# Encoder kernel on one core: the loading and splitting of x in another order, two blocks to a PSUM bank, two load queues

## The chip, the cores and the metric

The kernel runs on one core of a Trainium2 chip. The metric is the device time of one execution in microseconds; the time before is the median of three runs. The engines go by the names of the profile: PE is TensorE (PEld its weight loads), ACT is ScalarE, DVE is VectorE, POOL is GpSimd, SP is SyncE, which here issues most DMA transfers.

## The reference, cut to what matters

A two-layer encoder on 256 tokens of 1024 features, all in float32. Each layer is a half-step SwiGLU, a mixer (windowed attention beside a convolution module), a second half-step SwiGLU, and a gated embedding. The change touches only the very start of layer 0: x comes in, is scaled by the gain of the first norm and goes into the first SwiGLU product.

```python
def rms_norm(x, g, eps=1e-6):
    y = x * lax.rsqrt(jnp.mean(x * x, axis=-1, keepdims=True) + eps)
    return y * g

def swiglu(x, w_in, w_out):
    gate, up = jnp.split(x @ w_in, 2, axis=-1)
    return (jax.nn.silu(gate) * up) @ w_out

for i in range(DEPTH):
    h = x + 0.5 * swiglu(rms_norm(x, norm_ffn1[i]), w_ffn1_in[i], w_ffn1_out[i])
    ...
```

## The kernel before

**Layout.** Activations are kept transposed, features on the 128 partitions and the 256 tokens along the row. The 1024 features of x make eight blocks of 128 (`KD` = 8), counted 0 to 7. `x32` keeps x in float32 for the residual sum.

**Products.** Each matrix product is made of three: an operand is split into a high part and a low part, both in the float32r form of TensorE, and `mm3` (lines 311 to 313) adds high x high, low x high and high x low for every block. So x becomes `x0h` (ACT: x times the gain, rounded) and `x0l` (DVE: x times the gain minus `x0h`). A weight tile of 128 x 1024 goes through the same: it lands as `raw`, ACT casts it to `w_hi` (line 100), DVE subtracts to make `w_lo` (line 101). The factor 1/rms is applied after the product, so the products don't wait for it.

**Weights.** `Weights` loads units of 0.5 or 1 MB on SP's queue (line 76) into four `raw` buffers, and prepares tiles ahead of their use into seven `w_hi`/`w_lo` pairs. The incoming x (`x_ld`) takes one of the four `raw` buffers until its last block has been transposed. The first four units are 0.5 MB, one tile each; the units after them are 1 MB, two tiles each.

**The start.** x comes as four quarters of 256 columns (two blocks each) on SP's queue (line 166); the gains `rows_first` come on ACT's queue (line 180). TensorE transposes the gains into `ps_par`, and ACT copies them to `par`. Then, for each block: two transposes into PSUM (`ps_xt`, line 461), `x0h` on ACT (line 464), `x0l` on DVE (line 465); and two blocks later `keep_x` copies the block from PSUM to `x32` (line 456, ACT and DVE in turn). Each block has a PSUM tile of its own. The squares of x are summed on ACT and POOL (lines 396 to 400, `sq_acc`) and one matmul adds them over the partitions (`ps_stat`, line 409), after which 1/rms is made and the finished products may leave PSUM.

**What sets the order.** A scheduler orders each engine's instructions by priority and its own estimate of time, except where the code forbids it: in the block of line 450 ACT and DVE keep the order in which the code is written (`manual_schedule`). TensorE's order there is the scheduler's. Within one PSUM tile the framework makes an engine that writes wait for the engines that read, whichever part of the tile they use.

**The first product group.** It is "fresh": `pair` runs blocks 0 to 6 with the first tile (21 matmuls), blocks 0 to 6 with the second, and then block 7 with both (6 matmuls). PSUM has two pools: `mm_tile`, four tiles of one bank, and `at_tile`, two tiles of two banks.

Of the kernel before, what the change touches and what calls it, by code (L numbers as in the profile page):

```python
# [9 lines left out]
F32 = mybir.dt.float32  # L10
F32R = mybir.dt.float32r
AF = mybir.ActivationFunctionType
ALU = mybir.AluOpType
AX = mybir.AxisListType

P = 128
T = 256
D = 1024
KD = D // P
# [119 lines left out]
def encoder_kernel(ctx: ExitStack, tc: tile.TileContext, a: dict, out: bass.AP):  # L139
    nc = tc.nc  # L140
# [11 lines left out]
    def mm_tile(name):  # L152
        return mmp.tile([P, 512], F32, name=name, tag="mm")
# [5 lines left out]
    ident = const.tile([P, P], F32, name="ident")  # L159
    make_identity(nc, ident)  # L160

    x_ld = raw_pool.tile([P, 2, D], F32, name="x_ld", tag="raw")
    xv = a["x"][0].rearrange("(t p) d -> p t d", p=P)
    for i in range(4):
        s = slice(i * 256, (i + 1) * 256)
        nc.sync.dma_start(x_ld[:, :, s], xv[:, :, s])

    col = {}
    par = const.tile([P, 96], F32, name="par")
# [13 lines left out]
    def place_params(tile_, rows, c0):  # L183
        r0 = 0
        for name in rows:
            n = 1 if name in ("q_norm", "k_norm") else a[name].shape[1] // P
            col[name] = (c0 + r0, n)
            r0 += L * n
        ps = at_tile("ps_par")
        nc.tensor.transpose(ps[:, :r0], tile_[:r0, :], ident[:r0, :r0])  # L190
        nc.scalar.copy(out=par[:, c0 : c0 + r0], in_=ps[:, :r0])
        return c0 + r0
# [5 lines left out]
    ws = Weights(tc, raw_pool, w_pool)  # L198
# [101 lines left out]
    def pcol(name, l, k):  # L300
        c0, n = col[name]
        return par[:, c0 + l * n + k : c0 + l * n + k + 1]
# [32 lines left out]
    x32 = xp.tile([P, KD, T], F32, name="x32", tag="x32")  # L335
# [114 lines left out]
    with tc.manual_schedule(engines={mybir.EngineType.Activation, mybir.EngineType.DVE}):  # L450
        n_par = place_params(rows_first, ("norm_ffn1",), 0)
        xT = {}

        def keep_x(k):
            copy = nc.scalar.copy if k % 2 else nc.vector.tensor_copy
            copy(out=x32[:, k, :], in_=xT[k])  # L456

        for k in range(KD):
            xT[k] = (mm_tile if 2 <= k < 6 else at_tile)("ps_xt")[:, :T]
            for t in range(2):  # L460
                nc.tensor.transpose(xT[k][:, t * P : (t + 1) * P], x_ld[:, t, k * P : (k + 1) * P], ident)
            gain = pcol("norm_ffn1", 0, k)
            xh, xl = (x[:, k, :] for x in x_cur)
            nc.scalar.activation(out=xh, in_=xT[k], func=AF.Copy, scale=gain)
            nc.vector.scalar_tensor_tensor(
                out=xl, in0=xT[k], scalar=gain, in1=xh.bitcast(F32), op0=ALU.mult, op1=ALU.subtract
            )
            if k >= 2:
                keep_x(k - 2)
        ws.prep_upto(0)  # L470
        keep_x(KD - 2)
        keep_x(KD - 1)
        ws.prep_upto(1)
        for k in range(KD):
            stat.add(x32[:, k, :])
    r_cur = stat.finish(5)
# [599 lines left out]
```

## Time and profile before

| | us |
|---|---|
| median of three runs (1176.48 to 1177.78) | 1177.25 |
| the profiled execution | 1176.52 |
| its span, first to last instruction | 1174.7 |
| PE busy | 1156.8 (98%) |
| DVE busy | 813.6 (69%) |
| ACT busy | 614.2 (52%) |
| POOL busy | 88.5 (8%) |
| first product group starts | 10.76 |

Times in the trace count from the span's start. In the list of waits a row reads: who waited, for whom, us in total, how often, the longest. In the chain a row reads: start, length, what. In the timeline: start, length, engine, line, operation, output<-inputs, size, how many were merged, and in brackets how long the engine was idle before it and what ended that. Matmuls overlap, so their spacing is the difference of two starts, and not the length of one. The granted clock reads 1.00 throughout.

### The profile page before, as it was taken

What the parts mean: (1) busy time and instruction counts of PE and PEld (TensorE: products, weight loads), DVE (VectorE), ACT (ScalarE), POOL (GpSimd) and SP (SyncE); (2) the same over time, 40 slices, a digit from 0 to 9 for tenths busy, and PEclk for the clock granted to TensorE, in tenths of its full rate; (3) what the DMA queues carried; (4) which work ended last, traced back from release to release, by engine and by line L of the source; (5) the groups of instructions that cost most, each with busy time, mean ns of one, the idle gap of its engine ahead of it and who ended that gap; (6) DMA issues with size and microseconds to landing.
All of it is one profiled execution on the core that took longest, in us unless ns stands there. A gap on an engine that the chain in (4) does not pass through costs nothing.

```text
span 1174.7 us, 21809 instructions
## 1 busy us (share of the span) xinstructions
PE 1156.8 (98%) x9082; PEld 1121.5 (95%) x9082; DVE 813.6 (69%) x1214; ACT 614.2 (52%) x1033; POOL 88.5 (8%) x119
## 2 busy tenths in 40 slices
PE   7999999999999999999999999999999999999997
PEld 7999999998889999999999999999987999999997
DVE  5866656798667766656876666569976786666564
ACT  6644444676356544444664444457753564444443
POOL 3000001211002000001110000113000010000110
PEclk9999999999999999999999999999999999999999
DMA  8866556545074565556556464566522664654541
GB/s 252 265 229 209 167 178 200 179 147 141 2 249 161 189 200 175 171 165 214 188 166 204 156 205 152 170 213 193 145 72 68 219 224 159 201 168 144 192 144 37
DMA packets 195694, 202.99 MB, mean 173 GB/s; under 512 B 3731, under 2 KB 188899, under 8 KB 195596
## 3 DMA queue, kind: packets, MB, share of 16 engines
q1 hardware_dynamic: 195564, 201.60, 53.6%
q8 instruction: 71, 1.16, 0.4%
q14 instruction: 27, 0.22, 0.1%
q10 hardware_dynamic: 32, 0.01, 0.0%
HBM read 200.53 MB, written 1.06 MB: 172 GB/s over the span
## 4 chain that ended last, share of the span: by engine, by line
PE 96%; DVE 2%; DMA 1%; ACT 1%; issue 0%; SPq 0%; ACTq 0%
PE ps_gu L313 14%; PE ps_gu L311 14%; PE ps_gu L312 14%; PE ps_fo L313 7%; PE ps_fo L312 7%; PE ps_fo L311 7%; PE ps_g L311 3%; PE ps_g L313 3%; PE ps_g L312 3%; PE ps_co L847 2%; PE ps_s L755 1%; PE ps_c L311 1%; PE ps_pe L313 1%; PE ps_pe L312 1%; PE ps_pe L311 1%; PE ps_c L313 1%
## 5 line engine op out<-in xcount | busy, mean ns | idle before, releaser
L101 DVE TENSOR_TENSOR w_lo<-raw,w_hi 128x1024 fp32r<-128x1024 f32 (+1 forms) x368 | 440.9, 1202 | 241.5 <-ACT w_hi L100 237.4
L100 ACT CAST w_hi<-raw 128x1024 fp32r<-128x1024 f32 (+1 forms) x368 | 377.2, 1030 | 427.0 <-PE ps_gu L312 215.3
L313 PE MATMUL ps_fo<-h_hi,w_lo 128*128 128x256 f32 x704 | 198.6, 283 | 0.0
L312 PE MATMUL ps_fo<-h_lo,w_hi 128*128 128x256 f32 x704 | 198.6, 283 | 0.0
L311 PE MATMUL ps_fo<-h_hi,w_hi 128*128 128x256 f32 x704 | 198.6, 283 | 0.0
L313 PEld LDWEIGHTS ps_fo<-h_hi,w_lo 128*128 128x128 f32 x704 | 134.9, 192 | 0.0
L311 PEld LDWEIGHTS ps_fo<-h_hi,w_hi 128*128 128x128 f32 x704 | 134.9, 192 | 0.0
L312 PEld LDWEIGHTS ps_fo<-h_lo,w_hi 128*128 128x128 f32 x704 | 134.9, 192 | 0.0
L400 POOL TENSOR_TENSOR sq_acc<-sq_acc,sq 128x256 f32<-128x256 f32 x56 | 56.5, 1010 | 903.4 <-ACT sq L399 902.9
L311 PE MATMUL ps_gu<-x0h,w_hi 128*128 128x256 f32 x352 | 100.8, 286 | 2.1 <-ACT x L456 2.1
L607 DVE SCALAR_TENSOR_TENSOR y<-cpad,cw,y 128x256 f32<-128x256 f32 x240 | 101.1, 477 | 0.1
L313 PE MATMUL ps_gu<-x0h,w_lo 128*128 128x256 f32 x352 | 100.4, 285 | 0.2 <-DVE w_lo L101 0.2
L312 PE MATMUL ps_gu<-x0l,w_hi 128*128 128x256 f32 x352 | 100.2, 285 | 0.0
L311 PE MATMUL ps_gu<-xn0h,w_hi 128*128 128x256 f32 x352 | 99.8, 284 | 0.0
L312 PE MATMUL ps_gu<-xf0l,w_hi 128*128 128x256 f32 x352 | 99.8, 284 | 0.0
L312 PE MATMUL ps_gu<-xf1l,w_hi 128*128 128x256 f32 x352 | 99.8, 284 | 0.0
L311 PE MATMUL ps_gu<-xf0h,w_hi 128*128 128x256 f32 x352 | 99.7, 283 | 0.0
L311 PE MATMUL ps_gu<-xf1h,w_hi 128*128 128x256 f32 x352 | 99.7, 283 | 0.0
L313 PE MATMUL ps_gu<-xf0h,w_lo 128*128 128x256 f32 x352 | 99.6, 283 | 0.0
L313 PE MATMUL ps_gu<-xn0h,w_lo 128*128 128x256 f32 x352 | 99.6, 283 | 0.0
L312 PE MATMUL ps_gu<-xn0l,w_hi 128*128 128x256 f32 x352 | 99.6, 283 | 0.0
L313 PE MATMUL ps_gu<-xf1h,w_lo 128*128 128x256 f32 x352 | 99.6, 283 | 0.0
(222 smaller groups left out, 2718.6 us busy)
## 6 DMA issues: line engine op xcount, KB each, us to landing
raw<-in_w_ffn_in_dram SPq DMA_DIRECT2D x86, 1024.0 KB
raw<-in_w_in_dram SPq DMA_DIRECT2D x30, 1024.0 KB
raw<-in_w_ffn_out_dram SPq DMA_DIRECT2D x32, 896.0 KB
raw<-in_w_ffn_out_dram SPq DMA_DIRECT2D x16, 1024.0 KB
raw<-in_w_o_dram SPq DMA_DIRECT2D x8, 1024.0 KB
raw<-in_w_pe_gate_dram SPq DMA_DIRECT2D x8, 1024.0 KB
raw<-in_w_attn_out_dram SPq DMA_DIRECT2D x8, 512.0 KB
raw<-in_w_conv_out_dram SPq DMA_DIRECT2D x4, 1024.0 KB
```

What stands on the lines that cost most here:

```text
L100: nc.scalar.copy(out=hv[:, :, d0 : d0 + w], in_=src),
L101: nc.vector.tensor_tensor(out=lv[:, :, d0 : d0 + w], in0=src, in1=hv[:, :, d0 : d0 + w].bitcast(F32), op=ALU.subtract,),
L311: nc.tensor.matmul(ps, wh[:, k0 + k, cols], xh[:, kx, :], start=f, stop=False)
L312: nc.tensor.matmul(ps, wh[:, k0 + k, cols], xl[:, kx, :], start=False, stop=False)
L313: nc.tensor.matmul(ps, wl[:, k0 + k, cols], xh[:, kx, :], start=False, stop=e)
L400: nc.gpsimd.tensor_tensor(out=self.acc, in0=self.acc, in1=sq, op=ALU.add)
L607: nc.vector.scalar_tensor_tensor(out=y[:, i, :], in0=src, scalar=w, in1=y[:, i, :], op0=ALU.mult, op1=ALU.add)
L755: nc.tensor.matmul(ps[:, c, :], qT[v * HD : (v + 1) * HD, c, qb * P : (qb + 1) * P], kT[v * HD : (v + 1) * HD, :], start=True, stop=True,)
L847: nc.tensor.matmul(ps[:, c * T : (c + 1) * T], w[:, k, c * P : (c + 1) * P], x[:, k, :], start=k == 0, stop=k == KC - 1,)
```

## The change

Three edits, all ahead of the first product. (1) Quarters 0 and 2 of x are loaded on SP's queue, quarters 1 and 3 on ACT's, where `rows_first` now stands behind them. (2) Two blocks share a one-bank PSUM tile: blocks 0 and 1, 2 and 3, 4 and 5, 6 and 7; all four tiles come from `mm_tile`. (3) `keep_x` is gone: after the second weight tile has been prepared, four copies of two blocks each fill `x32`. The first weight tile is prepared after block 4, not after block 7.

```diff
--- before.py
+++ after.py
@@ -163,7 +163,7 @@
     xv = a["x"][0].rearrange("(t p) d -> p t d", p=P)
     for i in range(4):
         s = slice(i * 256, (i + 1) * 256)
-        nc.sync.dma_start(x_ld[:, :, s], xv[:, :, s])
+        (nc.sync if i % 2 == 0 else nc.scalar).dma_start(x_ld[:, :, s], xv[:, :, s])
 
     col = {}
     par = const.tile([P, 96], F32, name="par")
@@ -451,26 +451,24 @@
         n_par = place_params(rows_first, ("norm_ffn1",), 0)
         xT = {}
 
-        def keep_x(k):
-            copy = nc.scalar.copy if k % 2 else nc.vector.tensor_copy
-            copy(out=x32[:, k, :], in_=xT[k])
-
         for k in range(KD):
-            xT[k] = (mm_tile if 2 <= k < 6 else at_tile)("ps_xt")[:, :T]
+            if k % 2 == 0:
+                xT[k // 2] = mm_tile("ps_xt").rearrange("p (k t) -> p k t", k=2)
+            src = xT[k // 2][:, k % 2, :]
             for t in range(2):
-                nc.tensor.transpose(xT[k][:, t * P : (t + 1) * P], x_ld[:, t, k * P : (k + 1) * P], ident)
+                nc.tensor.transpose(src[:, t * P : (t + 1) * P], x_ld[:, t, k * P : (k + 1) * P], ident)
             gain = pcol("norm_ffn1", 0, k)
             xh, xl = (x[:, k, :] for x in x_cur)
-            nc.scalar.activation(out=xh, in_=xT[k], func=AF.Copy, scale=gain)
+            nc.scalar.activation(out=xh, in_=src, func=AF.Copy, scale=gain)
             nc.vector.scalar_tensor_tensor(
-                out=xl, in0=xT[k], scalar=gain, in1=xh.bitcast(F32), op0=ALU.mult, op1=ALU.subtract
+                out=xl, in0=src, scalar=gain, in1=xh.bitcast(F32), op0=ALU.mult, op1=ALU.subtract
             )
-            if k >= 2:
-                keep_x(k - 2)
-        ws.prep_upto(0)
-        keep_x(KD - 2)
-        keep_x(KD - 1)
+            if k == 4:
+                ws.prep_upto(0)
         ws.prep_upto(1)
+        for k in range(0, KD, 2):
+            copy = nc.scalar.copy if k % 4 else nc.vector.tensor_copy
+            copy(out=x32[:, k : k + 2, :], in_=xT[k // 2])
         for k in range(KD):
             stat.add(x32[:, k, :])
     r_cur = stat.finish(5)
```

In the rows below, names carry buffer numbers and "waits" lists the semaphores of the engine or DMA queue that a row waits for. TensorE at the start, before: ps_xt_107 to ps_xt_147 are blocks 0 to 7, one tile each, and ps_gu_202 is the first product group.

```order
L190 MATMUL ps_par_104<-ident_78,rows_first_89 128x16 [waits DMAHW0_49,Pool_49]
L461 MATMUL ps_xt_107<-ident_78,x_ld_83 128x128 [waits DMAHW1_49]
...
L461 MATMUL ps_xt_112<-ident_78,x_ld_83 128x128 [waits Activation_49]
...
L461 MATMUL ps_xt_117<-ident_78,x_ld_83 128x128 [waits DMAHW2_49]
...
L461 MATMUL ps_xt_123<-ident_78,x_ld_83 128x128 x2
L461 MATMUL ps_xt_129<-ident_78,x_ld_83 128x128 [waits DMAHW3_49]
...
L461 MATMUL ps_xt_135<-ident_78,x_ld_83 128x128 x2
L461 MATMUL ps_xt_141<-ident_78,x_ld_83 128x128 [waits DMAHW4_49,PE_49,Activation_49]
...
L461 MATMUL ps_xt_147<-ident_78,x_ld_83 128x128 [waits DVE_49]
...
L311 MATMUL ps_gu_202<-x0h_100,w_hi_159 128x256 [waits PE_49,Activation_49]
...
L313 MATMUL ps_gu_202<-x0h_100,w_lo_160 128x256 [waits DVE_49]
```

TensorE now: ps_xt_107, _116, _125 and _144 are the tiles of blocks 0 and 1, 2 and 3, 4 and 5, 6 and 7.

```order
L459 MATMUL ps_xt_107<-ident_78,x_ld_83 128x128 [waits DMAHW1_49,Pool_49]
...
L459 MATMUL ps_xt_116<-ident_78,x_ld_83 128x128 [waits DMAHW0_49]
...
L459 MATMUL ps_xt_125<-ident_78,x_ld_83 128x128 [waits DMAHW2_49]
...
L459 MATMUL ps_xt_144<-ident_78,x_ld_83 128x128 [waits DMAHW3_49]
...
L190 MATMUL ps_par_104<-ident_78,rows_first_89 128x16 [waits DMAHW5_49]
L459 MATMUL ps_xt_107<-ident_78,x_ld_83 128x128 [waits DVE_49]
...
L459 MATMUL ps_xt_116<-ident_78,x_ld_83 128x128 [waits DVE_49]
...
L459 MATMUL ps_xt_125<-ident_78,x_ld_83 128x128 [waits DVE_49]
...
L311 MATMUL ps_gu_194<-x0h_100,w_hi_136 128x256 [waits Activation_49]
...
L311 MATMUL ps_gu_194<-x0h_100,w_hi_136 128x256 [waits Activation_49]
L459 MATMUL ps_xt_144<-ident_78,x_ld_83 128x128 [waits DVE_49]
...
L311 MATMUL ps_gu_194<-x0h_100,w_hi_155 128x256 [waits Activation_49]
```

One even block of each quarter comes first, then the gains, then the odd blocks, each behind a wait for DVE; block 7 stands inside the first product group, after the first product of block 6, and ps_gu_194 takes its second weight tile (w_hi_155) behind it.

ACT up to the second weight cast, before:

```order
L180 DMA rows_first_89<-in_norm_ffn1_dram 16x128
...
L191 COPY par_88<-ps_par_104 128x16 [waits PE_49]
L464 ACTIVATE x0h_100<-ps_xt_107,par_88 128x256 [waits PE_49,Activation_49]
L464 ACTIVATE x0h_100<-ps_xt_112,par_88 128x256 [waits PE_49]
L464 ACTIVATE x0h_100<-ps_xt_117,par_88 128x256 [waits PE_49]
L464 ACTIVATE x0h_100<-ps_xt_123,par_88 128x256 [waits PE_49]
L456 COPY x32_99<-ps_xt_112 128x256 [waits DVE_49]
L464 ACTIVATE x0h_100<-ps_xt_129,par_88 128x256 [waits PE_49]
...
L464 ACTIVATE x0h_100<-ps_xt_141,par_88 128x256 [waits PE_49]
L464 ACTIVATE x0h_100<-ps_xt_147,par_88 128x256 [waits PE_49]
...
L100 CAST w_hi_159<-raw_153 128x1024 [waits DMAHW5_49]
...
L100 CAST w_hi_167<-raw_155 128x1024 [waits DMAHW6_49]
```

ACT now:

```order
L166 DMA x_ld_83<-in_x_dram 128x2x256 x2
L180 DMA rows_first_89<-in_norm_ffn1_dram 16x128
...
L191 COPY par_88<-ps_par_104 128x16 [waits PE_49]
L462 ACTIVATE x0h_100<-ps_xt_107,par_88 128x256 [waits Activation_49]
L462 ACTIVATE x0h_100<-ps_xt_107,par_88 128x256 [waits DVE_49,PE_49]
L462 ACTIVATE x0h_100<-ps_xt_116,par_88 128x256
L462 ACTIVATE x0h_100<-ps_xt_116,par_88 128x256 [waits DVE_49,PE_49]
L462 ACTIVATE x0h_100<-ps_xt_125,par_88 128x256
L100 CAST w_hi_136<-raw_130 128x1024 [waits DMAHW4_49]
L462 ACTIVATE x0h_100<-ps_xt_125,par_88 128x256 [waits DVE_49,PE_49]
...
L462 ACTIVATE x0h_100<-ps_xt_144,par_88 128x256 [waits DVE_49,PE_49]
L100 CAST w_hi_155<-raw_132 128x1024 [waits DMAHW6_49]
```

The copies to x32 have left this stretch, the first weight cast has moved ahead of blocks 5, 6 and 7, and the x0h of every odd block waits for DVE and PE.

ACT from the casts of the fifth unit (raw_195) and the sixth (raw_201) to ps_stat, now:

```order
L100 CAST w_hi_209<-raw_195 128x1024 [waits DMAHW1_49]
L399 ACTIVATE sq_171<-x32_99 128x256 [waits Pool_49]
L399 ACTIVATE sq_174<-x32_99 128x256 [waits DVE_49,Pool_49]
L100 CAST w_hi_215<-raw_201 128x1024 [waits DMAHW2_49]
L100 CAST w_hi_219<-raw_195 128x1024
L100 CAST w_hi_244<-raw_201 128x1024 [waits PE_49]
L399 ACTIVATE sq_177<-x32_99 128x256 [waits Pool_49]
L399 ACTIVATE sq_180<-x32_99 128x256 [waits Pool_49]
L100 CAST w_hi_299<-raw_207 128x1024 [waits DMAHW3_49,PE_49]
L399 ACTIVATE sq_183<-x32_99 128x256 [waits Pool_49]
...
L364 ACTIVATE sd_360<-ps_stat_358,eps6_95 128x256 [waits PE_49]
```

Before, six of the eight squares stood ahead of the cast of the fifth unit (there raw_203), two behind it, and none behind the casts of the sixth (raw_209):

```order
L399 ACTIVATE sq_179<-x32_99 128x256 [waits Pool_49]
L399 ACTIVATE sq_182<-x32_99 128x256 [waits Pool_49]
L399 ACTIVATE sq_185<-x32_99 128x256 [waits Pool_49]
L100 CAST w_hi_217<-raw_203 128x1024 [waits DMAHW1_49]
L399 ACTIVATE sq_188<-x32_99 128x256 [waits DVE_49,Pool_49]
L399 ACTIVATE sq_191<-x32_99 128x256 [waits Pool_49]
L100 CAST w_hi_223<-raw_209 128x1024 [waits DMAHW2_49]
L100 CAST w_hi_227<-raw_203 128x1024
```

Three of the eight squares (sq_177, sq_180, sq_183) have moved behind the cast of the sixth unit, w_hi_215.

SP's weight loads, now:

```order
L166 DMA x_ld_83<-in_x_dram 128x2x256 x2
L76 DMA raw_130<-in_w_ffn1_in_dram 128x8x128
...
L76 DMA raw_153<-in_w_ffn1_in_dram 128x8x128 [waits DMAHW4_49,DMAHW0_49,DVE_49]
L76 DMA raw_195<-in_w_ffn1_in_dram 128x8x256 [waits DMAHW2_49,DMAHW3_49,DMAHW1_49,PE_49]
L76 DMA raw_201<-in_w_ffn1_in_dram 128x8x256 [waits DMAHW6_49,DVE_49]
L76 DMA raw_207<-in_w_ffn1_in_dram 128x8x256 [waits DMAHW7_49,DVE_49]
```

The fourth unit (raw_153) now waits for DVE, that is for the w_lo of the first; the fifth (raw_195) has taken over the wait for PE, the release of x_ld. Before, the fourth had that wait. Beyond this stretch every engine's order is the same as before.

## Prediction

> **What bounds the kernel now.** I read the page first (busy shares, chain by engine), then TensorE's waits, then the chain and the timeline of the first 25 us, where all of the change lies.
>
> ```profile
> PE 1156.8 (98%) x9082; PEld 1121.5 (95%) x9082; DVE 813.6 (69%) x1214; ACT 614.2 (52%) x1033; POOL 88.5 (8%) x119
> PE 96%; DVE 2%; DMA 1%; ACT 1%; issue 0%; SPq 0%; ACTq 0%
> ```
>
> TensorE is busy for 98% of the span and is 96% of the chain that ended last. So a microsecond by which its stream of products starts later, or stands still, is a microsecond of the total; nothing behind it has slack to give it back. The waits of TensorE over the whole span (us in total, times, longest):
>
> ```profile
> PE ps_par L190 <- DMA rows_first<-in_norm_ffn_dram: 3.3, 1, 3.3
> PE ps_var L876 <- ACT ysq L871: 3.2, 2, 1.6
> PE ps_gu L311 <- ACT x L456: 2.1, 1, 2.1
> ```
>
> Two of the three largest lie ahead of the first product. The chain there (start, length, what):
>
> ```profile
> 1.72 4.83 DMA x_ld<-in_x_dram
> 6.59 0.70 PE ps_xt L461 x2
> 7.32 0.90 ACT x0h L464 x2
> ...
> 9.22 0.26 ACT x L456
> 9.48 0.95 ACT w_hi L100
> 10.46 1.24 DVE w_lo L101
> 11.74 0.58 PE ps_gu L313
> ```
>
> The third quarter of x lands at 6.55, blocks 4 to 7 go through ScalarE (x0h, two kept copies, then the cast of the first weight tile), VectorE makes w_lo, and at 11.74 the first product that needs all of it starts. From there TensorE runs on:
>
> ```profile
> 10.76 0.58 PE L311 MATMUL ps_gu<-x0h,w_hi 128*128 128x256 f32 x1 [2.09 <-ACT x L456]
> ...
> 14.26 0.38 PE L312 MATMUL ps_gu<-x0l,w_hi 128*128 128x256 f32 x1
> 14.47 0.28 PE L313 MATMUL ps_gu<-x0h,w_lo 128*128 128x256 f32 x1
> 14.59 0.28 PE L311 MATMUL ps_gu<-x0h,w_hi 128*128 128x256 f32 x1
> ...
> 15.55 0.28 PE L313 MATMUL ps_gu<-x0h,w_lo 128*128 128x256 f32 x1
> ...
> 24.31 0.59 PE L409 MATMUL ps_stat<-sq_acc,ones_d 128*128 128x256 f32 x2
> ```
>
> Three things to see. Products start every 0.213 us until 14.47 and every 0.12 us after it, 3.7 us from the first one. The row at 15.55 is the 24th product, the first that needs the second tile's w_lo: it did not wait. At 24.31, 8.76 us later, comes ps_stat, which needs the sum of squares of x: it did not wait either. These are my three marks: 11.74, 15.55, 24.31.
>
> **The change part by part.**
>
> *Two load queues.* Two quarters of x move to ScalarE's queue, each with its issue, ahead of rows_first (the gains) and the table load (all three hidden, since par comes later still); SyncE reaches the weights two issues sooner. (The first two rows are windows of half a microsecond; their last three columns are granted clock, DMA share and GB/s.)
>
> ```profile
> 2.50:3.00 0.50, 0.00 (x0) 0.00 (x0) 0.00 (x0) 0.00 (x0) 0.00 (x0) 1.00 1.02 306
> 5.00:5.50 0.50, 0.50 (x5) 0.49 (x3) 0.28 (x1) 0.50 (x2) 0.00 (x0) 1.00 0.62 147
> 0.71 0.46 ACTq L180 DMA_DIRECT2D rows_first<-in_norm_ffn_dram  x1
> 0.72 1.98 SPq L166 DMA_DIRECT2D x_ld<-in_x_dram  x4
> 3.29 0.26 PE L190 MATMUL ps_par<-ident,rows_first 16*128 16x16 f32 x1 [3.29 <-DMA rows_first<-in_norm_ffn_dram]
> 3.92 1.97 PE L461 MATMUL ps_xt<-ident,x_ld 128*128 128x128 f32 x8 [0.38 <-DMA x_ld<-in_x_dram]
> 6.59 2.07 PE L461 MATMUL ps_xt<-ident,x_ld 128*128 128x128 f32 x8 [0.70 <-DMA x_ld<-in_x_dram]
> ```
>
> Issues cost 0.5 us each (1.98 for four). One queue already moves 306 GB/s at 2.5 us, with a dip to 147 around 5. The third quarter lands at 6.55 and the fourth by 7.5 (blocks 6 and 7 follow in the row at 6.59 without a wait). Now the last quarters of both queues should land together. Lowest: the dip fills, and 1.05 MB at 306 GB/s from 2.0 lands at about 5.6. Highest: 7.5. I take 7.0, between the two old landings, since the bytes are the same. [...] No run here shows two queues on x yet.
>
> What is lost is earliness. rows_first had landed by 3.29; now it stands behind two quarters on its queue, and in TensorE's order ps_par stands behind one block of every quarter. No x0h can start without par, so blocks 0 to 3, which ran while the rest of x was still loading, no longer do. From 7.0: the transposes of blocks 4 and 6, four starts 0.22 apart (0.9), ps_par to copy 0.29, copy and start 0.2: the first x0h at 8.4 instead of 4.72.
>
> *Two blocks in one bank.* In the new order an odd block's transposes wait for VectorE's x0l of the even block in the same bank, and ScalarE keeps the order of blocks.
>
> ```profile
> 3.58 0.17 ACT L191 COPY par<-ps_par 128x16 f32<-128x16 f32 x1 [1.09 <-PE ps_par L190]
> 4.72 1.69 ACT L464 ACTIVATE x0h<-ps_xt,par 128x256 fp32r<-128x256 f32 x4 [0.97 <-PE ps_xt L461]
> 5.22 1.27 DVE L465 SCALAR_TENSOR_TENSOR x0l<-ps_xt,par,x0h 128x256 fp32r<-128x256 f32 x3 [5.22 <-ACT x0h L464]
> 9.35 1.08 ACT L100 CAST w_hi<-raw 128x1024 fp32r<-128x1024 f32 x1
> ```
>
> x0h used to come every 0.41 us (four in 1.69, each 0.47). Now one pair takes a round trip: x0h to x0l 0.50, x0l and signal 0.52, a pair of transposes up to the next x0h 0.73 (6.59 to 7.32), then 0.41 to the next even block: 2.16 instead of 0.82. Block 4's x0h starts at 8.4 + 2 x 2.16 = 12.7, the first weight cast at 13.1. Cast start to the w_lo product was 9.35 to 11.74, 2.39: so that product starts at 15.5, **3.75 us later**. The first weight itself is hidden: its load is issued two issues earlier, and it had landed by 9.35 before.
>
> *Copies later.* The kept copies go from eight to four and off the path ahead of the first cast (0.26 twice on the chain above); already in the sum, since I counted none. They now stand between weight casts, under the 3 us of products that the second weight tile feeds; without that cover the two on ScalarE would cost about 0.5 each, twice the 0.26.
>
> *Block 7 inside the first products.* Its transposes stand after the 19th product and its x0h ahead of the second weight cast. From 15.5, 17 products: slow until 3.7 us after the first one (14.2 + 3.7 = 17.9), 11 at 0.213, then 6 at 0.12: 18.6. Transposes to x0h 0.73, x0h to cast 0.41, cast to w_lo product 2.39: the 24th product at 22.1 instead of 15.55, **6.5 us later**; TensorE idles for nearly 3 us before it.
>
> *Squares and weight loads.* The squares start after the copies, and three of the last now stand behind three casts that need the sixth weight unit. SyncE loads the fourth unit when the first w_lo is done (15.4), the fifth when x_ld is free (block 7's transposes, 19.2) and the sixth when the second w_lo is done (22.0).
>
> ```profile
> 14.54 1.06 ACT L100 CAST w_hi<-raw 128x1024 fp32r<-128x1024 f32 x1 [0.58 <-DMA raw<-in_w_ffn_in_dram]
> 16.05 3.08 POOL L400 TENSOR_TENSOR sq_acc<-sq_acc,sq 128x256 f32<-128x256 f32 x3 [0.23 <-ACT sq L399]
> 20.47 4.13 ACT L100 CAST w_hi<-raw 128x1024 fp32r<-128x1024 f32 x4 [0.89 <-DMA raw<-in_w_ffn_in_dram]
> ```
>
> Two 1 MB units took 14.54 to 20.47, 3.0 each; a small load needed 2.5 from issue to use (0.71 to 3.29). Fourth, half a MB: 15.4 + 2.5 + 1.5 = 19.4, hidden, since its products come 49 products after the mark at 22.1, near 28. Fifth: 19.2 + 2.5 + 3.0 = 24.7. Sixth: 27.7. Three casts (4.13 for four) 3.1: 30.8. Square 0.4, three additions on GpSimd 3.1: 34.3. TensorE would be at ps_stat at 22.1 + 8.76 = 30.9. So it stands 3.4 us and ps_stat comes at 34.3, **10.0 us later** than 24.31. If all of that is hidden the delay stays at 6.5. Behind ps_stat the order on every engine is the old one and all of it is late alike; the weights that feed TensorE were ahead of it (its list has no wait for them after 11.74), so nothing more is lost.
>
> Sum: the profiled execution took 1176.5 (span 1174.7 and 1.8 around it); 1176.5 + 10.0 = **1186.5**. The median shown, 1177.25, is 0.7 above that execution.
>
> **The rivals.**
>
> *The sum of squares is in time.* The sixth unit lands about 3 us sooner, or the casts leave room. Then only the first two delays count: 1176.5 + 6.5 = 1183.0. For it: the additions ended 2.7 us ahead of ps_stat before (last at 19.34 + 2.29 by the same chain). Against: the cast of the sixth unit waited for its load before, too (0.89 in the row at 20.47).
>
> ```profile
> 19.34 2.29 POOL L400 TENSOR_TENSOR sq_acc<-sq_acc,sq 128x256 f32<-128x256 f32 x2 [0.21 <-ACT sq L399]
> ```
>
> *The slow pace returns.* If 3 us without products bring back the 0.213 pace for another 3.7 us, 17 products cost 0.093 more each, 1.6 us. After the first gap this is swallowed by the wait at ps_stat; after ps_stat it counts: 1188.1. The trace has no such gap; after its longest in the middle, 1.61 us, the pace was as before, about 0.22 for these fp32 products:
>
> ```profile
> 320.89 1.03 PE L847 MATMUL ps_ao<-o,raw 128*128 128x256 f32 x4
> 323.95 1.13 PE L876 MATMUL ps_var<-ysq,ones_c 128*128 128x256 f32 x4 [1.61 <-ACT ysq L871]
> ```
>
> [...]
>
> *Not slower.* The waits inside a bank cost nothing, because VectorE is done by the time TensorE gets there. Then x0h keeps its 0.41 pace, the first cast comes 2.05 after the first x0h, and the mark of 11.74 holds if that x0h starts by 7.3, so x by 5.9. With x at 5.6: 1176.2, within 0.2%. It decides at x by 5.9 and no wait in a bank; the built order has the wait, and x0l needs x0h, which needs par, which comes after everything. Faster by 0.2% (2.35 us, about what a measurement of this kernel can tell from no change) is out of reach of this mechanism.
>
> **How the numbers follow.** Forecast 62%; squares in time 15%; slow pace returns 15%; not slower 5%; above that 3%. Low end: x at 5.6 (-1.4) and the squares in time (-3.5): 1181.6. High end: x at 7.5 (+0.5), the slow pace (+1.6): 1188.6, and 0.7 for the median: 1189.3. Slower 93%, same 5%, faster 2%.
>
> **What would show it.** Right: first x0h after 8, x0h in pairs some 2.1 us apart, transposes waiting for VectorE's x0l; first w_lo product near 15.5; a wait of TensorE for w_hi and w_lo near 20; a wait of ps_stat for GpSimd's additions of about 3 us; the rest of the trace the same, shifted. Wrong: x0h at 0.41 pace, par before 5, no wait at ps_stat, or a gap given back later on.

## The result, and the profile after

The changed kernel takes 1188.43 us (median of four runs, 1187.95 to 1189.4) against 1177.3 for the kernel before on the same chip: ratio 1.0096 (1.0079 to 1.0114), 11.1 us slower. The forecast was 1186.5, range 1181.6 to 1189.3. The profiled execution took 1188.31 with a span of 1186.5, 11.8 more than the span before; the readings below are of it.

The page after, busy shares and chain by engine:

```profile
PE 1160.4 (98%) x9082; PEld 1124.0 (95%) x9082; DVE 815.5 (69%) x1212; ACT 614.2 (52%) x1031; POOL 88.3 (7%) x119
PE 95%; DMA 1%; ACT 1%; DVE 1%; POOL 1%; issue 0%; SPq 0%; ACTq 0%; POOLq 0%
```

PE's busy time rose by 3.6 us with the same 9082 matmuls: some ran at a slower clock (0.50 and 0.51 in two windows below). The rest of the 11.8 is standing still. PE's waits after (us in total, times, longest):

```profile
PE ps_xt L459 <- DMA x_ld<-in_x_dram: 5.3, 2, 5.1
PE ps_xt L459 <- DVE x0l L463: 4.2, 3, 1.5
...
PE ps_stat L409 <- POOL sq_acc L400: 3.2, 1, 3.2
...
PE ps_gu L311 <- ACT w_hi L100: 1.3, 1, 1.3
PE ps_gu L313 <- DVE w_lo L101: 1.2, 2, 0.8
```

The second row is the round trip inside a bank, which the kernel before did not have; the third is the late sum of squares; the last two are the weights that stand behind block 7 (of the 1.2, only 0.8; the other 0.46 is the first w_lo product). In the timeline, ACT's first rows:

```profile
8.04 0.47 ACT L462 ACTIVATE x0h<-ps_xt,par 128x256 fp32r<-128x256 f32 x1
9.82 0.84 ACT L462 ACTIVATE x0h<-ps_xt,par 128x256 fp32r<-128x256 f32 x2 [1.30 <-PE ps_xt L459]
11.98 0.84 ACT L462 ACTIVATE x0h<-ps_xt,par 128x256 fp32r<-128x256 f32 x2 [1.33 <-PE ps_xt L459]
12.71 1.04 ACT L100 CAST w_hi<-raw 128x1024 fp32r<-128x1024 f32 x1
```

x0h starts at 8.04 instead of 4.72, and comes in pairs about 2.16 us apart, ACT idle 1.3 us in each. The three marks of the prediction (11.74, 15.55 and 24.31 before) now, with the additions that the last one waits for:

```profile
15.07 0.58 PE L313 MATMUL ps_gu<-x0h,w_lo 128*128 128x256 f32 x1 [0.46 <-DVE w_lo L101]
...
20.33 0.39 PE L311 MATMUL ps_gu<-x0h,w_hi 128*128 128x256 f32 x1 [1.26 <-ACT w_hi L100]
...
21.59 0.58 PE L313 MATMUL ps_gu<-x0h,w_lo 128*128 128x256 f32 x1 [0.76 <-DVE w_lo L101]
...
23.92 5.00 POOL L400 TENSOR_TENSOR sq_acc<-sq_acc,sq 128x256 f32<-128x256 f32 x4 [22.16 <-ACT sq L399]
31.03 4.07 POOL L400 TENSOR_TENSOR sq_acc<-sq_acc,sq 128x256 f32<-128x256 f32 x3 [2.11 <-ACT sq L399]
35.15 1.22 PE L409 MATMUL ps_stat<-sq_acc,ones_d 128*128 128x256 f32 x2 [3.15 <-POOL sq_acc L400]
35.81 0.78 PE L311 MATMUL ps_gu<-x0h,w_hi 128*128 128x256 f32 x1
36.38 0.41 PE L312 MATMUL ps_gu<-x0l,w_hi 128*128 128x256 f32 x1
```

The same in the chain (start, length, what), which now runs through ACT, DVE and POOL up to ps_stat:

```profile
1.22 5.17 DMA x_ld<-in_x_dram
...
8.04 0.48 ACT x0h L462
...
33.51 1.59 POOL sq_acc L400
35.15 1.22 PE ps_stat L409 x2
```

The delays are 3.33, 6.04 and 10.84 us. After ps_stat the products are 0.41 us long again, the form of the slow pace (0.28 at full pace). PE in windows (busy, matmuls, granted clock, DMA share, GB/s):

```profile
18.00:21.40 3.40, 1.58 (x11) 0.99 0.39 121
21.40:24.80 3.40, 3.21 (x15) 0.51 1.08 366
24.80:28.20 3.40, 3.40 (x30) 1.00 1.09 349
31.60:35.00 3.40, 0.40 (x4) 1.00 0.26 74
35.00:38.40 3.40, 3.25 (x13) 0.50 0.31 65
```

The granted clock is 0.51 and 0.50 in two windows, each of which follows a window in which PE was busy for less than half. The slow stretch after ps_stat costs (35.81 - 35.15) instead of 0.24 to the next product, 0.42, and some 12 products at 0.213 instead of 0.12 up to 38.48, 1.1 to 1.2: about 1.6. With 10.84 that is 12.4; about 0.6 is given back later (0.4 of it at ps_co, whose wait fell from 2.1 to 1.7), which leaves the 11.8.

### The profile page after: what moved, and what is told of

Same layout as the page of the kernel before. It is cut to its first block, busy times and chain, and to the rows that moved or that the text cites. A ratio compares the mean times of both kernels' runs of the same rounds, so it can differ in the third digit from the quotient of the medians.

```text
span 1186.5 us, 21810 instructions
## 1 busy us (share of the span) xinstructions
PE 1160.4 (98%) x9082; PEld 1124.0 (95%) x9082; DVE 815.5 (69%) x1212; ACT 614.2 (52%) x1031; POOL 88.3 (7%) x119
## 3 DMA queue, kind: packets, MB, share of 16 engines
HBM read 200.53 MB, written 1.06 MB: 170 GB/s over the span
## 4 chain that ended last, share of the span: by engine, by line
PE 95%; DMA 1%; ACT 1%; DVE 1%; POOL 1%; issue 0%; SPq 0%; ACTq 0%; POOLq 0%
PE ps_gu L313 14%; PE ps_gu L311 14%; PE ps_gu L312 14%; PE ps_fo L313 7%; PE ps_fo L312 7%; PE ps_fo L311 7%; PE ps_g L311 3%; PE ps_g L313 3%; PE ps_g L312 3%; PE ps_co L845 2%; PE ps_s L753 1%; PE ps_c L311 1%; PE ps_pe L313 1%; PE ps_pe L312 1%; PE ps_pe L311 1%; PE ps_c L313 1%
```

## The experiments

The verdicts below compare medians with the kernel before on the same chip, 1176.8 to 1176.9. The changed kernel itself was measured apart from them, beside 1177.3, so a difference of two medians between an experiment and its 1188.43 is uncertain by some 0.5 us; the second figure in such places takes each against its own before.

**1. Two load queues alone.**

```
before.py:
-        nc.sync.dma_start(x_ld[:, :, s], xv[:, :, s])
+        (nc.sync if i % 2 == 0 else nc.scalar).dma_start(x_ld[:, :, s], xv[:, :, s])
```

> The kernel before with the two load queues alone; every block keeps its own PSUM tile and the copies stay early. Theory (late gains cost): the gains land behind two quarters of x, so par is late and the first x0h starts near 8.0, as in the changed kernel (8.04), not at 4.72. From there ScalarE needs 8 x 0.42 for the x0h and 3 x 0.38 for copies, 4.5 us, then 2.39 from the first weight cast to the first w_lo product: near 14.9 instead of 11.74. No later wait is added, because squares and weight casts keep their order. Total 1177.3 + 3.2 = 1180.5. Rival (the gains were hidden behind the load of x anyway): w_lo product by 12, total 1177.3, within 0.2%.

Measured: 1180.15 us, ratio 1.0025 (1.0014 to 1.0036). In its timeline:

```profile
7.86 0.17 ACT L191 COPY par<-ps_par 128x16 f32<-128x16 f32 x1 [4.29 <-PE ps_par L190]
8.54 1.57 ACT L464 ACTIVATE x0h<-ps_xt,par 128x256 fp32r<-128x256 f32 x4 [0.51 <-PE ps_xt L461]
...
14.81 0.58 PE L313 MATMUL ps_gu<-x0h,w_lo 128*128 128x256 f32 x1 [0.19 <-DVE w_lo L101]
...
28.18 0.60 PE L409 MATMUL ps_stat<-sq_acc,ones_d 128*128 128x256 f32 x2
```

The size is what was worked out: the first w_lo product is 3.07 late, and ps_stat comes without a wait, 3.87 late. The 0.8 between the two is the slow pace at the start, which here lasts from 13.83 to 19.43. The queue edit by itself is a loss of 3.3 us. That all of it is the late gains is not shown: x is late too (the first transposes start at 5.50 instead of 3.92), and the first x0h waited 0.51 us behind par for transposes that TensorE ran after ps_par. Experiment 7, with two queues and the gains first, still loses 2.3 us, though it moves a cast as well.

**2. Two blocks in a bank alone.** Pair tiles, copies of two blocks one pair later, both weight tiles after all blocks; one queue, gains early.

```
before.py:
+            if k % 2 == 0:
+                xT[k // 2] = mm_tile("ps_xt").rearrange("p (k t) -> p k t", k=2)
+            src = xT[k // 2][:, k % 2, :]
...
-            if k >= 2:
-                keep_x(k - 2)
+            if k % 2 and k >= 3:
+                keep_x(k // 2 - 1)
```

> The kernel before with two blocks to a bank alone: one load queue with the gains beside it, copies of two blocks one pair later, both weight tiles prepared after all blocks. On TensorE the order becomes block 0, ps_par, 2, 4, 1, 6, 3, 5, 7. Theory (the round trip inside a bank costs): first x0h at 4.7 as before, but block 1 stands behind block 4 and its x (6.55), and each odd block behind the x0l of the even one; eight x0h end near 13, the first weight cast starts near 13.6 and the first w_lo product near 16.0, 4.3 us late. Squares and copies keep their place, all later work is late alike, so ps_stat does not wait: total 1177.3 + 4.3 = 1181.6. Rival (the waits in a bank are covered by the load of x): w_lo product by 13, total within 1.3 us of 1177.3.

Measured: 1182.99 us, ratio 1.0053 (1.0038 to 1.0068). PE's waits and marks:

```profile
PE ps_xt L463 <- DVE x0l L467: 5.0, 3, 2.1
PE ps_gu L311 <- ACT w_hi L100: 1.5, 1, 1.5
```

```profile
18.08 0.58 PE L313 MATMUL ps_gu<-x0h,w_lo 128*128 128x256 f32 x1 [0.52 <-DVE w_lo L101]
...
30.85 0.60 PE L409 MATMUL ps_stat<-sq_acc,ones_d 128*128 128x256 f32 x2
```

The round trips are real: 5.0 us of PE waiting for x0l (1.03 before block 3, 2.07 and 1.94 before blocks 5 and 7), and no wait behind the first w_lo product up to ps_stat. The size was too small by 2 us (w_lo product at 18.08, not 16.0). About half of that are the copies of a pair, which now stand inside the round trip: VectorE's ahead of the x0l of block 4, ScalarE's ahead of the x0h of block 6. The x0h of blocks 1, 3, 5 and 7 start at 7.75, 9.92, 12.68 and 15.31, so a round trip took 2.17 without a copy in it, and 2.76 and 2.63 with one. Another 0.4 is the first x0h, at 5.15 instead of 4.7; the rest is open.

**3. The changed kernel with the gains loaded first.** Only the place of the four x loads differs: after `rows_first` instead of before it.

> The changed kernel with the gains issued on ScalarE's queue ahead of the two quarters of x; the rest as changed. Theory (late gains, then pairs in a bank, then late squares, each adds): par is ready before 5, the first x0h starts near 4.9, and two pairs later (1.97 each in the changed kernel) block 4's x0h at 8.9 instead of 11.98. Everything behind it moves up by about 3.1: first w_lo product at 12.0, ps_stat at 32.0, with its wait of about 3 us and the slow pace behind it unchanged. Total 1188.4 - 3.1 = 1185.3. Rival (the pair round trips wait for x, not for the gains): the first x0h is early, but block 4's x0h stays near 11 or later and the total within 1 us of 1188.4.

Measured: 1186.74 us, ratio 1.0082 (1.0066 to 1.0099); 1.7 below the changed kernel (1.2 by the two ratios to before) where 3.1 was expected.

```profile
5.13 0.47 ACT L463 ACTIVATE x0h<-ps_xt,par 128x256 fp32r<-128x256 f32 x1
7.65 0.84 ACT L463 ACTIVATE x0h<-ps_xt,par 128x256 fp32r<-128x256 f32 x2 [2.05 <-PE ps_xt L460]
9.82 0.84 ACT L463 ACTIVATE x0h<-ps_xt,par 128x256 fp32r<-128x256 f32 x2 [1.33 <-PE ps_xt L460]
...
12.90 0.58 PE L314 MATMUL ps_gu<-x0h,w_lo 128*128 128x256 f32 x1 [0.46 <-DVE w_lo L101]
...
33.63 0.70 PE L410 MATMUL ps_stat<-sq_acc,ones_d 128*128 128x256 f32 x2 [3.05 <-POOL sq_acc L401]
```

The first x0h is early as expected, but the second comes 2.5 us later: block 1's transposes stand behind those of blocks 2 and 4, which wait for x. The expectation also read the row at 11.98 in the changed kernel as block 4; it starts with block 3, whose x0h is now at 9.82. Neither theory was right alone. With the gains early, the order of the blocks on PE takes over as the reason for the late start; the round trips after it, and the wait at ps_stat, are as in the changed kernel.

**4. ps_stat two weight tiles later.**

```
after.py:
-    r_cur = stat.finish(5)
+    r_cur = stat.finish(7)
```

> The changed kernel with ps_stat two weight tiles later in TensorE's order (48 products, about 5.8 us at 0.12). Theory (the late sum of squares costs its wait and the slow pace after it): the sum is ready at 35.1, ps_stat is reached at about 37.5, so neither the wait of 3.15 nor the 17 products at 0.213 (1.4 us) remain: total 1188.4 - 4.6 = 1183.8. If the slow pace after ps_stat has another cause than the wait: 1185.2. Rival (the wait only moves: the products' PSUM tiles can't be emptied without r_x, and TensorE waits for a tile instead): 1188.4.

Measured: 1188.28 us, ratio 1.0097 (1.0082 to 1.0112): no gain. PE's wait at ps_stat is gone; this is the row in its place, and ACT's rows behind it:

```profile
PE ps_gu L311 <- ACT sd L364: 1.6, 1, 1.6
```

```profile
44.38 1.05 ACT L100 CAST w_hi<-raw 128x1024 fp32r<-128x1024 f32 x1 [6.10 <-DMA raw<-in_w_ffn_in_dram]
45.45 1.28 ACT L364 ACT_TABLE_LOAD   x1
46.74 0.47 ACT L364 ACTIVATE sd<-ps_stat,eps 128x256 f32<-128x256 f32 x1
```

ps_stat ran at 39.37, but its square root `sd` stood behind a weight cast that waited 6.10 us for its load, and PE stood 1.56 us for a PSUM tile that can't be emptied without it. That is half of the 3.15. In the profiled execution the rest can be placed: the 24th product came 0.87 later than in the changed kernel (22.46), and the products stayed slow until 27.74 instead of 24.75, 14 of them at 0.093 more, 1.3. So 0.87, 1.3 and 1.56 stand against 3.15 and 1.6 (the wait and the slow pace after it): 1.0 gained, and this span is 0.9 shorter. It was the fastest of its four executions, and the median shows none of it. So this run tells little about the price of the wait, and the next one was made to take away its cause instead.

Two windows of PE matter further down; the first is at the slow pace, which lasted on behind it, the second holds the wait of 1.56:

```profile
14.10:17.50 3.40, 2.94 (x14) 1.00 0.27 79
44.79:48.20 3.41, 1.85 (x15) 1.00 1.10 351
```

**5. Squares taken from PSUM.** Each pair's two squares follow the first x0h of the next pair, in ACT's 1.3 us of idle time; the copies stay late and ps_stat keeps its place among the products.

```
after.py:
+            if k % 2 == 0 and k:
+                for j in range(2):
+                    stat.add(xT[k // 2 - 1][:, j, :])
         ws.prep_upto(1)
+        for j in range(2):
+            stat.add(xT[KD // 2 - 1][:, j, :])
...
-        for k in range(KD):
-            stat.add(x32[:, k, :])
```

> The changed kernel with the squares taken straight from the PSUM tiles, each pair's two behind the first x0h of the next pair (where ScalarE waits for the round trip anyway), the last two behind the third weight cast; copies stay late. ps_stat keeps its place among TensorE's products. Theory (in the changed kernel the late squares cost the wait of 3.15 at ps_stat, and the slow pace after it is the price of that wait): additions end near 25, ps_stat runs without a wait some 10 us behind the 24th product, near 32, and the products after it keep 0.12: total 1188.4 - 3.15 - 1.4 = 1183.8. If the slow pace has another cause: 1185.2. Rival (what ends last at ps_stat is the weights of the sixth unit, and the sum of squares only rides along): TensorE waits for the weights instead and the total stays near 1188.4.

Measured: 1184.4 us, ratio 1.0059 (1.0044 to 1.0074), 4.0 below the changed kernel (3.6 by the two ratios).

```profile
22.06 0.42 PE L313 MATMUL ps_gu<-x0h,w_lo 128*128 128x256 f32 x1 [0.76 <-DVE w_lo L101]
23.07 2.41 POOL L400 TENSOR_TENSOR sq_acc<-sq_acc,sq 128x256 f32<-128x256 f32 x2 [4.95 <-ACT sq L399]
32.42 0.59 PE L409 MATMUL ps_stat<-sq_acc,ones_d 128*128 128x256 f32 x2
```

```profile
35.00:38.40 3.40, 3.40 (x31) 1.00 0.20 56
```

The 24th product is 0.5 later than in the changed kernel, the additions end at 25.5, ps_stat does not wait, and the clock stays at 1.00 behind it. So the late squares, with the slow pace after them, are worth about 4 us of the 11, and the sixth unit's weights did not hold PE in their place.

**6. Idle products in the wait.** Eight float32 products of ones into the unused half of ps_stat's tile; their results are not read.

```
after.py, Stat.done:
+            if self.fill:
+                for k in range(self.fill):
+                    nc.tensor.matmul(ps[:, T:], ones_d, x32[:, k % KD, :], start=True, stop=True)
             nc.tensor.matmul(ps[:, :T], ones_d, self.acc, start=True, stop=True)
```

> The changed kernel with eight idle products of ones and kept blocks of x (two records of 0.22 each) written to the unused half of ps_stat's tile; two of them land among the earlier products, six directly ahead of ps_stat, 2.6 us of its 3.15 wait. Their results are not read. Theory (the pace falls to 0.213 because TensorE was idle): ps_stat itself still comes near 35, but the products after it keep 0.12, the 17 slow products are gone: total 1188.4 - 1.4 = 1187.0, to be read from the trace, since it is within the spread. Rival (the pace falls whenever float32 products or a switch of operands come in, or with time): 17 products at 0.213 after ps_stat as in the changed kernel, 1188.4 or, by a longer ps_stat, 1189.

Measured: 1188.4 us, ratio 1.0096 (1.0081 to 1.0111). The timeline, and the same window as above:

```profile
33.25 2.75 PE L412 MATMUL ps_stat<-x,ones_d 128*128 128x256 f32 x12
35.84 0.59 PE L413 MATMUL ps_stat<-sq_acc,ones_d 128*128 128x256 f32 x2
```

```profile
35.00:38.40 3.40, 3.40 (x25) 1.00 0.20 54
```

The cause is shown: with PE kept busy, the clock stays at 1.00 where the changed kernel was granted 0.50. ps_stat came 0.7 later in this execution: the 24th product was 0.46 late already (22.05), and the idle products ran until 36.00, past the end of the additions at 35.54. Without the slow pace the products behind it still run 0.9 ahead of those of the changed kernel, up to 359 us; there 0.6 of the lead is lost at ps_wo, which now waits for VectorE. The span is 0.2 shorter and the median does not move, so a gain in time is not shown; the 1.4 expected is about the spread of the runs.

**7. A candidate.** The kernel before with the gains first, then two queues, and the first weight tile prepared after block 4; own tiles and early copies.

> The kernel before with two load queues, the gains issued first on ScalarE's, and the first weight tile prepared after block 4; every block in its own tile, early copies. Theory: with all of x landed near 6.5 and the gains early, the first x0h stays near 5, the third and fourth quarters no longer come one after the other, and the first weight cast stands ahead of three x0h and three copies (2.4 us): first w_lo product near 10.5 instead of 11.74, total 1177.3 - 1.2 = 1176.1. Rival (the weight itself is late, or the later blocks then hold the products up): w_lo product at 11.5 or later, total 1177.3 or above, up to 1178 where squares behind the cast of the sixth unit make ps_stat wait.

Measured: 1179.19 us, ratio 1.0020 (1.0010 to 1.0030): slower than before.

```profile
9.18 1.08 PE L462 MATMUL ps_xt<-ident,x_ld 128*128 128x128 f32 x4 [1.83 <-DMA x_ld<-in_x_dram]
13.22 0.55 PE L312 MATMUL ps_gu<-x0h,w_hi 128*128 128x256 f32 x1 [2.96 <-ACT x L457]
...
13.78 0.41 PE L314 MATMUL ps_gu<-x0h,w_lo 128*128 128x256 f32 x1
```

The rival held: the first w_lo product starts at 13.78, 2.0 later than before. The last quarter of x was in use only at 9.18, and the first weight cast had waited 1.28 for its load. ScalarE's queue issues its two quarters from 1.21 to 2.25, and SyncE's starts on the weights at 1.73, so x and the first weights are issued side by side; before, all of x was issued ahead of any weight and the last blocks started by 7.5. The copies that free the banks then end late too. How much is the queues' and how much the early cast's was not separated. No version here beats the kernel before.

## Why the prediction was right, point by point

**Late gains and the round trip (first mark).** Forecast +3.75, measured +3.33. The pace of 2.16 per pair was exact (9.82 to 11.98). Blocks 4 and 6, the last of x that the gains wait behind, were first used at 6.4 and 6.9 where 7.0 was taken for both; the first x0h came at 8.04 instead of 8.4, and that is the difference. (The 5.6 of the prediction's low end is a slip: 1.05 MB at 306 GB/s from 2.0 is 5.4.) Alone, the queues cost 3.3 us and the shared banks 6.2; the changed kernel without its late squares is 7.5 above before, 2 less than their sum. The cast after block 4 leaves blocks 5 to 7 behind it, and block 7 then takes some of that back; how the 2 us divide was not measured.

**Block 7 inside the products (second mark).** Forecast +6.5, measured +6.04, and 0.42 of the 0.46 between them is the first mark's. From the first mark to the second it took 6.52 where 6.6 was forecast. The idle time was 2.0 and not nearly 3, in two pieces (1.26 for w_hi, 0.76 for w_lo), since products of block 6 and of the second tile ran in between.

**The sum of squares (third mark).** Forecast +10.0, measured +10.84. The wait was 3.15 where 3.4 was forecast, and experiment 5 shows its cause. The term that was mis-sized is the last three additions: 4.07 us where 3.1 was taken, from a row of before (3.08 for three). VectorE worked for 3.48 of those 4.07 us, and for 1.06 of the 3.08:

```profile
31.03:35.10 4.07, 3.48 (x3) 0.99 0.36 109
```

```profile
16.05:19.13 3.08, 1.06 (x2) 1.00 1.05 339
```

So an addition on GpSimd took 1.36 us beside VectorE's 86% and 1.03 beside 34%, and in experiment 5 one beside an idle VectorE took 0.72. VectorE's share alone does not give the size, though: two additions took 1.48 each beside 64% (before, 12.86 to 15.81) and two 1.20 each beside 100% (experiment 5, 23.07 to 25.48). What made the additions longer was not shown.

**The slow pace (a rival at 15%).** This is the step that failed: the prediction left the return of the slow pace out of its sum, and the 15% was the author's estimate. The slow pace came back at ps_stat and cost about 1.6 us, as the rival had it: the largest part of the 1.8 between the forecast delay of 10.0 and the 11.8 of the profiled execution (0.84 more is ps_stat itself, and 0.6 was given back). Experiment 6 shows that idle time is its cause: from 31.50 to 35.00 PE was busy for 3.50 us there and for 0.49 in the changed kernel, and the clock in the window behind it was 1.00 and 0.50. The argument rested on a gap of 1.61 us with unchanged pace; it should have weighed how much of a fixed window is idle, not how long one gap is. The times at which the pace changed point to such windows, about 3.4 us long by an estimate from these rows: in the changed kernel the clock went up at 24.8 and again at 38.4, 13.6 apart, four times 3.4; in the run with the gains first the products changed pace at 21.04, 24.44, 34.64 and 38.05, which is 3.40, three times 3.40 and 3.41 apart. There the first products behind the wait at ps_stat, up to 34.64, still ran at full pace. The prediction's own sum had a gap of 3.4 at ps_stat and gave it no price. In the changed kernel a window in which PE was busy for 1.58 of 3.40 us was followed by a clock of 0.51; in experiment 4 one with 1.85 of 3.41 busy was followed by the full pace, a product every 0.12 us. The trace of before does not read 1.00 to its end either: behind its last transposes on PE, at 1169.98, the clock was 0.79 in the microsecond from 1171 and 0.50 in the next.

**The other rivals.** "Squares in time" did not happen in the changed kernel and would have cost 7.5 (experiment 5), not the 6.5 forecast. The difference is again the slow pace, here after the first gap: the 24th product was 6.51 late and ps_stat 8.11, and without a wait at ps_stat nothing swallows it. "Not slower" needed x by 5.9 and no wait in a bank; x came at 6.4 to 6.9 and PE waited 4.2 us for x0l.

## What to carry to other kernels

Before moving a small load behind a large one, ask who waits for the small one: here the edit that put 8 KB of gains behind x on its queue cost 3.3 us by itself, and in the changed kernel loading them first gave back 1.2 to 1.7. Two blocks in one PSUM bank joined writer and readers into a round trip here, 2.16 us a pair, with PE waiting 4.2 us in all, so pack a bank only where TensorE has other work, and keep sums whose only reader is TensorE ahead of casts that wait for loads (about 4 us here). When pricing a new gap on TensorE, add the slow pace that may follow it (about 1.6 us here), and judge by the idle share of the windows around the gap as well as by its length.

## What was not expected of the hardware

- A window of 3.4 us with PE busy for 46% (1.58 of 3.40) was followed by a granted clock of 0.51; one at 54% (1.85 of 3.41, from 44.79 in experiment 4) was not: the products behind it kept 0.12 us.
- How busy a window must be for the pace to rise stays open. At the slow pace of the start, 2.94 of 3.40 busy was followed by the full pace in the changed kernel (14.6 to 18.0) and by more of the slow pace in experiment 4 (14.10 to 17.50). The column of the granted clock reads 1.00 in both windows, so this first slow pace must be read from the spacing of the products.
- With two queues the loads reached 385 GB/s in slices of a quarter microsecond near 5 us, where one queue reached 350 at most in the first 10 us. That is not owed to the second queue: SyncE's alone moved 384 GB/s on average from 65.75 to 67.5 us in the kernel before. The last quarter of x was first used at 6.9, 8.0 and 9.2 us in the changed kernel and in experiments 3 and 7, all with two queues. Experiments 3 and 7 issue x and the gains in the same order at the same times, so the issue order does not explain the 1.2 between them; each is one profile, and the cause stays open.
